# Grouped-query attention on one core: a static instruction plan re-fitted to hand-over times read from a trace

## Chip, cores and metric

The kernel runs on 1 core of a Trainium2 chip. The metric is device time in microseconds (us) for one execution; several executions of each kernel are compared. Runs are "fast" with a granted TensorE clock of 0.995 to 1.0. The time is about 1.8 us longer than the span of a profile (385.81 us against 384.0 in the profiled run of before), so times are compared with times and spans with spans.

## The reference

```
q: (8, 8, 1024, 64), k and v: (8, 2, 1024, 64), float32, randn * 0.1
for each of 2 kv heads g, its 4 query heads:
    scores = q @ k^T / sqrt(64)
    attn   = exp(scores - max); attn = attn / (sum(attn) + 1e-8)
    output = attn @ v
```

There are 128 jobs (batch, query head, half of the queries; 512 queries each), each with 8 blocks of 128 keys: 1024 score tiles of 128 x 512.

## The kernel before

Each score tile is one matmul (0.2155 us apart on TensorE). Its exponential is made in one of two ways. **A tiles** go to ScalarE, two at a time. **D tiles** go to VectorE, one by one, which builds an approximate exponential out of bit operations and corrects ten tiles at once with a chain of four steps: mask ("and", VectorE), line (GpSimd), product and sum (VectorE). Then TensorE multiplies each tile with V (an output block of four matmuls, 0.123 us) and VectorE normalises each finished job. In PSUM there are two double banks for A, two single banks for D, two for outputs.

The order on each engine is fixed at build time. A greedy function simulates the engines with constant costs and always takes the operation that can start first; the sorted list is the program. The split between A and D is not a parameter: it comes out of this simulation.

```
QK, PV, P1, NORM = 0.216, 0.1225, 0.603, 0.555
EXP = (0.05, 0.4268)
FOUR, TWO, POOL_ONE = (0.09, 0.133), (0.05, 0.27), (0.25, 0.43)
COST = {"and": FOUR, "line": POOL_ONE, "prod": TWO, "add": TWO}
FROM_PE, FROM_PV, FROM_ACT, FROM_DVE, FROM_POOL = 0.21, 0.16, 0.165, 0.10, 0.15
LIVE_A, LIVE_D, PENDING, PER_JOB, LEAD, RAMP, AHEAD, FIRST_PV = 28, 5, 16, 2, 6, 6, 0.0, 2.0
AHEAD_D, EXTRA, LAST = 0, 0, 6
...
    if job_a < nj:                      # a score for ScalarE
        t = ...max(pe, bank free, data loaded)
            best = min(best or (INF,), (t - AHEAD, 1, "qk", 0, t))
    if job_d < nj and job_d <= job_a + lead + 1 and pending < PENDING:   # one for VectorE
        if cur or live["D"] < LIVE_D:
            t = max(pe, min(bank), loaded(job_d))
            best = min(best or (INF,), (t - AHEAD_D, 2, "qk", 1, t))
...                                     # output blocks, normalisations, chain steps likewise
        if len(o["cells"]) == A_CELLS[o["slot"]] or ...:
            act = max(act, pe + FROM_PE)
            ops.append((act, "exp", a_id, tuple(o["cells"])))
            act += EXP[0] + EXP[1] * len(o["cells"])
            a_free[o["slot"]] = act + FROM_ACT
```

The constants that begin with FROM are the hand-over times: how long after the end of an engine's step the plan lets another engine use its result. PENDING is the number of D tiles that may be begun and not finished. Transfers on GpSimd's queue are placed by planned time too, out of the way of the chains' line steps:

```
POOL_DMA = 1.0
def at_pool(t, f, *args):
    for first, last in chains:          # planned starts of the line steps
        if first - POOL_DMA < t < last:
            t = last + 0.01
    at(t, f, *args)
...
# cast(): a GpSimd transfer that also waits for the last score issued so far ("pace")
```

The softmax here doesn't subtract the row's maximum and nothing guards it: scores larger than these inputs give would overflow.

Of the kernel before, what the change touches and what calls it, by code (L numbers as in the profile page):

```python
# [19 lines left out]
def part(step, m):  # L20

    n = step[-1]
    return slice(0, m) if not n.isdigit() else slice(m * int(n) // PARTS, m * (int(n) + 1) // PARTS)


def make_plan(nj, nkc):
# [6 lines left out]

    QK, PV, P1, NORM = 0.216, 0.1225, 0.603, 0.555
    EXP = (0.05, 0.4268)
    FOUR, TWO, POOL_ONE = (0.09, 0.133), (0.05, 0.27), (0.25, 0.43)
    COST = {"and": FOUR, "line": POOL_ONE, "prod": TWO, "add": TWO}
    FROM_PE, FROM_PV, FROM_ACT, FROM_DVE, FROM_POOL = 0.21, 0.16, 0.165, 0.10, 0.15
    LIVE_A, LIVE_D, PENDING, PER_JOB, LEAD, RAMP, AHEAD, FIRST_PV = 28, 5, 16, 2, 6, 6, 0.0, 2.0
    INF = 1e9  # L40
    AHEAD_D, EXTRA, LAST = 0, 0, 6
    FIRST_TURN, FIRST_LOAD, EACH_LOAD = 2.4, 4.5, 4.2
# [9 lines left out]
    p1q, chainq, normq, cur = [], [], [], []  # L52
# [4 lines left out]
    def loaded(j):  # L57
        h = j // 2
        if not h:
            return FIRST_TURN * (j % 2)  # L60
        return FIRST_LOAD + EACH_LOAD * (h - 1 if h < 4 else h)

    def first_free(slots):
        return min(range(len(slots)), key=lambda s: slots[s])


    while normed < nj:
        best = None
        while job_a < nj and not todo[job_a]:
            job_a += 1  # L70
        lead = min(LEAD, job_a // RAMP)
        job_d = max(job_d, job_a + lead)
        while job_d < nj and (
            taken[job_d] >= PER_JOB + EXTRA * (job_d >= nj - LAST)
            or not todo[job_d]
        ):
            job_d += 1
        if job_a < nj:
            t = INF
            if open_a is not None:  # L80
                t = max(pe, open_a["t"], loaded(job_a))
            elif live["A"] < LIVE_A:
                t = max(pe, min(a_free), loaded(job_a))
            if t < INF:
                best = min(best or (INF,), (t - AHEAD, 1, "qk", 0, t))
        if job_d < nj and job_d <= job_a + lead + 1 and pending < PENDING:
            if cur or live["D"] < LIVE_D:
                t = max(pe, min(bank), loaded(job_d))
                if t < INF:
                    best = min(best or (INF,), (t - AHEAD_D, 2, "qk", 1, t))  # L90
        for i, s in enumerate(open_jobs):
            for c in rem[s]:
                at = max(pe, FIRST_PV, ready.get(s * nkc + c, INF))
                if at < INF:
                    best = min(best or (INF,), (at, 3 + i, "pv", (s, c)))
        if len(open_jobs) < O_BANKS and next_job < nj:
            at = min(ready.get(next_job * nkc + c, INF) for c in range(nkc))
            at = max(pe, FIRST_PV, min(obank_free), at)
            if at < INF:
                best = min(best or (INF,), (at, 3 + len(open_jobs), "open", next_job))  # L100
        for q, p, kind in ((normq, 0, "norm"), (p1q, 1, "p1")):
            if q:
                best = min(best or (INF,), (max(dve, q[0][0]), p, kind, 0))

        for i, (at, _, _, step) in enumerate(chainq):
            if CHAIN[step] in ON_POOL:
                at = max(at, pool, two_end)
            else:
                at = max(at, dve, pool)
            best = min(best or (INF,), (at, 2 + i, "chain", i))  # L110
        if cur and job_d >= nj and not p1q:
            best = min(best or (INF,), (dve, 9, "flush", 0))
        t, _, kind, arg = best[:4]
        if kind == "qk":
            t = best[4]
            pe = t + QK
            j = job_d if arg else job_a
            cell = j * nkc + todo[j].pop(0)
            if not arg:
                if open_a is None:  # L120
                    slot = first_free(a_free)
                    a_id += 1
                    live["A"] += 1
                    open_a = {"slot": slot, "t": a_free[slot], "cells": []}
                    a_free[slot] = INF
                o = open_a
                ops.append((t, "qk", cell, "A", a_id, o["slot"], len(o["cells"])))
                o["cells"].append(cell)
                home[cell] = ("A", a_id)
                if len(o["cells"]) == A_CELLS[o["slot"]] or not any(todo[job_a:]):  # L130
# [4 lines that stand above are left out]
                    uses[("A", a_id)] = len(o["cells"])  # L135
                    for x in o["cells"]:
                        ready[x] = act + FROM_ACT
                    open_a = None
            else:
                taken[j] += 1  # L140
                k = first_free(bank)
                bank[k] = INF
                pending += 1
                ops.append((t, "qk", cell, "D", k, 0, 0))
                p1q.append((pe + FROM_PE, cell, k))
        elif kind == "open":
            o = first_free(obank_free)
            obank[arg] = o
            obank_free[o] = INF
            open_jobs.append(arg)  # L150
            rem[arg] = list(range(nkc))
            next_job += 1
        elif kind == "pv":
            s, c = arg
            cell = s * nkc + c
            opens = len(rem[s]) == nkc
            rem[s].remove(c)
            done = not rem[s]
            ops.append((t, "pv", s, cell, opens, done, obank[s]))
            pe = t + PV  # L160
            h = home[cell]
            uses[h] -= 1
            if not uses[h]:
                live[h[0]] -= 1
            if done:
                open_jobs.remove(s)
                normq.append((pe + FROM_PV, s))
        elif kind == "norm":
            s = normq.pop(0)[1]
            ops.append((t, "norm", s))  # L170
            dve = t + NORM
            obank_free[obank[s]] = dve + FROM_DVE
            normed += 1
        elif kind == "p1":
            _, cell, k = p1q.pop(0)
            if not cur:
                d_id += 1
                live["D"] += 1
            ops.append((t, "p1", cell, k, d_id, len(cur)))
            dve = t + P1  # L180
            bank[k] = dve + FROM_DVE
            cur.append(cell)
            home[cell] = ("D", d_id)
            if len(cur) == GROUP:
                chainq.append((dve, d_id, cur, 0))
                cur = []
        elif kind == "flush":
            chainq.append((dve, d_id, cur, 0))
            cur = []
        else:  # L190
            _, g, cells, step = chainq.pop(arg)
            ops.append((t, "chain", g, len(cells), CHAIN[step]))
            name = CHAIN[step]
            fixed, each = COST[name.rstrip("0123456789")]
            end = t + fixed + each * len(cells[part(name, len(cells))])
            if name in ON_POOL:
                pool = end
            else:
                dve = two_end = end
            if step + 1 < len(CHAIN):  # L200
                at = end
                if (name in ON_POOL) != (CHAIN[step + 1] in ON_POOL):
                    at += FROM_POOL if name in ON_POOL else FROM_DVE
                chainq.insert(arg, (at, g, cells, step + 1))
            else:
                pending -= len(cells)
                uses[("D", g)] = len(cells)
                for x in cells:
                    ready[x] = dve + FROM_DVE
# [4 lines left out]
def kernel(  # L214
# [40 lines left out]

    jobs = [(b, h, side) for b in range(B) for h in range(H) for side in range(2)]
    plan = make_plan(len(jobs), NKC)
    starts = {}
    for op in plan:
# [391 lines left out]
```

## Time and profile before

| | before |
|---|---|
| time, median (range of 3) | 385.43 us (385.39 to 386.04) |
| span of the profiled run | 384.0 us |
| ScalarE / TensorE / VectorE / GpSimd busy | 98% / 95% / 92% / 45% |
| exponentials on ScalarE, D tiles, chains | 404, 216, 22 |

All three large engines are nearly full.

### The profile page before, as it was taken

What the parts mean: (1) busy time and instruction counts of PE and PEld (TensorE: products, weight loads), DVE (VectorE), ACT (ScalarE), POOL (GpSimd) and SP (SyncE); (2) the same over time, 40 slices, a digit from 0 to 9 for tenths busy, and PEclk for the clock granted to TensorE, in tenths of its full rate; (3) what the DMA queues carried; (4) which work ended last, traced back from release to release, by engine and by line L of the source; (5) the groups of instructions that cost most, each with busy time, mean ns of one, the idle gap of its engine ahead of it and who ended that gap; (6) DMA issues with size and microseconds to landing.
All of it is one profiled execution on the core that took longest, in us unless ns stands there. A gap on an engine that the chain in (4) does not pass through costs nothing.

```text
span 384.0 us, 12026 instructions
## 1 busy us (share of the span) xinstructions
PE 365.6 (95%) x5172; PEld 233.6 (61%) x5172; DVE 353.8 (92%) x548; ACT 374.6 (98%) x409; POOL 174.4 (45%) x147
## 2 busy tenths in 40 slices
PE   8879898999999999999999999999999999998995
PEld 7425464666666666666666666666666666564664
DVE  4779998999999999999999999999999999989982
ACT  5999999999999999999999999999999999999995
POOL 5584535718244371563718245271643627040420
PEclk9999999999999999999999999999999999999999
DMA  8988988697756848585676759468675765711213
GB/s 137 135 152 135 130 154 124 129 147 140 113 109 132 140 103 139 101 156 103 139 131 120 130 106 152 96 126 137 105 124 123 138 102 119 126 56 29 57 56 84
DMA packets 102485, 45.48 MB, mean 118 GB/s; under 512 B 63792, under 2 KB 100976, under 8 KB 101184
## 3 DMA queue, kind: packets, MB, share of 16 engines
q1 hardware_dynamic: 82096, 31.21, 36.1%
q0 software_dynamic: 19712, 13.18, 32.3%
q8 instruction: 40, 0.66, 0.7%
q10 hardware_dynamic: 624, 0.33, 0.3%
q14 instruction: 13, 0.11, 0.1%
HBM read 25.17 MB, written 27.00 MB: 136 GB/s over the span
## 4 chain that ended last, share of the span: by engine, by line
ACT 86%; PE 10%; DVE 2%; issue 1%
ACT p_ring L477 86%; PE aps L466 4%; PE ops L538 4%; PE ops L409 1%; PE dps L466 1%; DVE pd L527 1%; DVE ost L554 0%; DVE y L525 0%; DVE z L512 0%; DVE rec L551 0%; PE dps L382 0%; PE dps L428 0%; PE ops L428 0%; PE aps L382 0%; DVE blank L288 0%
## 5 line engine op out<-in xcount | busy, mean ns | idle before, releaser
L477 ACT ACTIVATE p_ring<-aps 128x1024 bf16<-128x1024 f32 x404 | 371.8, 1067 | 1.4 <-PE aps L466 1.2
L466 PE MATMUL aps<-qT,kset 128*128 128x512 bf16 x808 | 239.9, 378 | 13.0 <-ACT p_ring L477 12.4
L538 PEld LDWEIGHTS <-p_ring 128*128 128x128 bf16 x3232 | 140.1, 98 | 64.0
L538 PE MATMUL ops<-vset,p_ring 128*128 128x65 bf16 x3232 | 154.6, 194 | 0.0
L491 DVE TENSOR_SCALAR pd<-dps 128x512 uint16<-128x512 f32 x216 | 138.6, 683 | 7.0 <-PE dps L466 6.7
L516 POOL TENSOR_SCALAR y<-z 128x5120 f16<-128x5120 uint16 (+1 forms) x22 | 96.4, 4383 | 70.0 <-DVE rec L551 48.7
L466 PEld LDWEIGHTS <-kset 128*128 128x128 bf16 x1024 | 79.7, 97 | 56.4 <-issue 25.8
L323 POOL DMA_DIRECT2D scr_q<-in_q_dram x63 | 39.1, 621 | 83.5 <-PE dps L466 44.3
L466 PE MATMUL dps<-qT,kset 128*128 128x512 bf16 x216 | 76.4, 379 | 0.0
L525 DVE TENSOR_TENSOR y<-z,y 128x5120 f16<-128x5120 uint16 (+1 forms) x22 | 61.0, 2772 | 1.1 <-POOL y L516 1.1
L527 DVE TENSOR_TENSOR pd<-pd,y 128x5120 uint16<-128x5120 uint16 (+1 forms) x22 | 60.9, 2769 | 0.1
L554 DVE TENSOR_TENSOR ost<-ops,rec 128x256 f32<-128x256 f32 x128 | 54.3, 425 | 4.4
L538 PEld LDWEIGHTS <-pd 128*128 128x128 bf16 x864 | 42.8, 98 | 24.7 <-DVE ost L554 2.2
L538 PE MATMUL ops<-vset,pd 128*128 128x65 bf16 x864 | 52.2, 194 | 0.3
L512 DVE TENSOR_SCALAR z<-pd 128x5120 uint16<-128x5120 uint16 (+1 forms) x22 | 32.3, 1467 | 0.5
L551 DVE RECIPROCAL rec<-ops 128x4 f32<-128x4 f32 x128 | 22.6, 176 | 9.6 <-PE ops L538 8.2
L323 POOL DMA_DIRECT2D scr_k<-in_k_dram x15 | 9.8, 656 | 39.9 <-PE aps L466 33.0
L356 POOL DMA_DIRECT2D vset<-in_v_dram x32 | 24.9, 784 | 0.0
L409 PE MATMUL ops<-blank 128*128 128x128 bf16 x40 | 5.3, 313 | 1.1 <-DVE blank L288 1.1
L409 PEld LDWEIGHTS <-blank 128*128 128x128 bf16 x40 | 4.4, 149 | 1.1 <-DVE blank L288 1.1
L363 POOL DMA_DIRECT2D kset<-kset x6 | 4.1, 684 | 0.0
L420 ACT ACT_TABLE_LOAD x1 | 1.3, 1283 | 1.8 <-issue 1.8
(23 smaller groups left out, 10.2 us busy)
## 6 DMA issues: line engine op xcount, KB each, us to landing
out_dram<-ost SPq DMA_DIRECT2D x63, 256.0 KB, 2.9
scr_q<-in_q_dram POOLq DMA_DIRECT2D x63, 128.0 KB, 3.5
kset<-kT SPq DMA_DIRECT2D x60, 64.0 KB, 3.1
vset<-in_v_dram POOLq DMA_DIRECT2D x32, 64.0 KB, 3.9
scr_k<-in_k_dram POOLq DMA_DIRECT2D x15, 128.0 KB, 3.7
qT<-scr_q SPq DMA_TRANSPOSE x63, 3.5
kset<-kset POOLq DMA_DIRECT2D x6, 128.0 KB, 4.3
fq<-in_q_dram ACTq DMA_DIRECT2D x2, 128.0 KB, 3.3
```

The source lines that it names most:

```text
L323: dma = nc.gpsimd.dma_start(out=scr.rearrange("(p f) -> p f", f=1024), in_=src.rearrange("(p s) d -> p (s d)", s=1024 // D),)
L356: nc.gpsimd.dma_start(out=vsets[b % 2][:, g, two * NHC : (two + 1) * NHC, 0:D], in_=v[b, g].rearrange("(c p two) d -> two p c d", p=128, t ...
L466: last_score[0] = nc.tensor.matmul(dst, lhsT=ksets[b % 2][:, h // HPG, side, c * 128 : (c + 1) * 128], rhs=qT[(b, h)], start=True, stop=Tr ...
L477: act = nc.scalar.activation(out=pt[:, 0:m], in_=psum.pop(("A", n))[:, 0:m], func=AF.Exp, scale=scale)
L491: nc.vector.tensor_scalar(out=groups[g][:, slot], in0=psum.pop(cell), scalar1=bits_scale, scalar2=bits_bias, op0=ALU.mult, op1=ALU.add,)
L512: eng.tensor_scalar(out=z, in0=pd, scalar1=0x7F, scalar2=None, op0=ALU.bitwise_and)
L516: eng.tensor_scalar(out=y, in0=z, scalar1=CURVE_A / 128.0, scalar2=CURVE_B, op0=ALU.mult, op1=ALU.add,)
L525: eng.tensor_tensor(out=y, in0=z, in1=y, op=ALU.mult)
L527: eng.tensor_tensor(out=pd, in0=pd, in1=y, op=ALU.add)
L538: nc.tensor.matmul(ops_of[s][:, qs, :], lhsT=p_of[cell][:, qs * 128 : (qs + 1) * 128], rhs=vsets[b % 2][:, h // HPG, c, :], start=opens an ...
L551: nc.vector.reciprocal(out=rec, in_=o[:, :, D])
L554: nc.vector.tensor_tensor(out=stage[(b, h)][:, :, side, :], in0=o[:, :, 0:D], in1=rec.unsqueeze(2).to_broadcast([128, NQS, D]), op=ALU.mult,)
```

## The change

The intent is to let the plan's hand-over times be those that a trace shows between TensorE, VectorE and GpSimd, and to let a ScalarE score wait up to 0.06 us for its bank rather than have TensorE begin something else.

```
-    FOUR, TWO, POOL_ONE = (0.09, 0.133), (0.05, 0.27), (0.25, 0.43)
+    FOUR, TWO, POOL_ONE = (0.20, 0.133), (0.05, 0.27), (0.25, 0.417)
-    FROM_PE, FROM_PV, FROM_ACT, FROM_DVE, FROM_POOL = 0.21, 0.16, 0.165, 0.10, 0.15
-    LIVE_A, LIVE_D, PENDING, PER_JOB, LEAD, RAMP, AHEAD, FIRST_PV = 28, 5, 16, 2, 6, 6, 0.0, 2.0
+    FROM_PE, FROM_PV, FROM_ACT, FROM_DVE, FROM_POOL = 0.21, 0.20, 0.165, 0.135, 0.06
+    LIVE_A, LIVE_D, PENDING, PER_JOB, LEAD, RAMP, AHEAD, FIRST_PV = 28, 5, 16, 2, 6, 6, 0.06, 2.0
-                chainq.append((dve, d_id, cur, 0))
+                chainq.append((dve + 0.11, d_id, cur, 0))        # in both places
```

More of the change, by code (lines that the diff above doesn't have):

```diff
@@ L184, in make_plan @@
             if len(cur) == GROUP:
-                chainq.append((dve, d_id, cur, 0))
+                chainq.append((dve + 0.11, d_id, cur, 0))
                 cur = []
         elif kind == "flush":
-            chainq.append((dve, d_id, cur, 0))
+            chainq.append((dve + 0.11, d_id, cur, 0))
             cur = []
```

## The prediction

> **What bounds the kernel now.** I read the busy line first, then the groups, the chain that ended last, the waits, and last a few microseconds of the timeline.
>
> ```profile
> span 384.0 us, 12026 instructions
> PE 365.6 (95%) x5172; PEld 233.6 (61%) x5172; DVE 353.8 (92%) x548; ACT 374.6 (98%) x409; POOL 174.4 (45%) x147
> ```
>
> ScalarE (ACT) is busy 98% of the span, TensorE 95% and VectorE 92%. Nothing here has much room, so the question is which engine sets the pace and by how much the others disturb it.
>
> ```profile
> L477 ACT ACTIVATE p_ring<-aps 128x1024 bf16<-128x1024 f32 x404 | 371.8, 1067 | 1.4 <-PE aps L466 1.2
> L466 PE MATMUL aps<-qT,kset 128*128 128x512 bf16 x808 | 239.9, 378 | 13.0 <-ACT p_ring L477 12.4
> L491 DVE TENSOR_SCALAR pd<-dps 128x512 uint16<-128x512 f32 x216 | 138.6, 683 | 7.0 <-PE dps L466 6.7
> L516 POOL TENSOR_SCALAR y<-z 128x5120 f16<-128x5120 uint16 (+1 forms) x22 | 96.4, 4383 | 70.0 <-DVE rec L551 48.7
> ```
>
> 404 exponentials of two score tiles each on ScalarE, 216 score tiles on VectorE (808 + 216 = 1024), in 22 chains. ScalarE's idle time is only 1.4 us, but this figure hides something: one exponential lasts 1067 ns and yet 404 of them occupy 371.8 us, 920 ns each, because the next begins before the last has ended. A late score first eats this overlap, and only then appears as idle. From the start times in the trace: the shortest distance between two starts is 0.903 us, half of the 403 distances lie between 0.903 and 0.910, the mean is 0.920. Against 0.905 (my choice for an undisturbed one) the sum of excess is 6.2 us. That is nearly all that better feeding can win at this split.
>
> ```profile
> 105.11 23.81 ACT p_ring L477 x26
> 128.99 23.90 ACT p_ring L477 x26
> 152.93 23.86 ACT p_ring L477 x26
> 176.86 23.80 ACT p_ring L477 x26
> 200.71 23.91 ACT p_ring L477 x26
> ```
>
> In the chain in order of time, runs of 26 exponentials take about 23.86 us, 0.918 each; undisturbed they would take 26 x 0.905 = 23.53. So the loss is spread evenly, 0.3 us in each run. Where it comes from:
>
> ```profile
> 170.34 4.47 POOL L516 TENSOR_SCALAR y<-z 128x5120 f16<-128x5120 uint16 x1
> 170.34 0.42 DVE L554 TENSOR_TENSOR ost<-ops,rec 128x256 f32<-128x256 f32 x1
> 170.59 0.13 PEld L466 LDWEIGHTS <-kset 128*128 128x128 bf16 x2
> 170.62 0.60 PE L466 MATMUL aps<-qT,kset 128*128 128x512 bf16 x2
> 170.68 2.49 DVE L491 TENSOR_SCALAR pd<-dps 128x512 uint16<-128x512 f32 x4
> ...
> 171.05 0.41 PE L538 MATMUL ops<-vset,p_ring 128*128 128x65 bf16 x8
> ...
> 171.41 0.38 PE L466 MATMUL dps<-qT,kset 128*128 128x512 bf16 x1
> 171.63 0.59 PE L466 MATMUL aps<-qT,kset 128*128 128x512 bf16 x2
> ```
>
> TensorE takes its work in the fixed order that the plan chose. The eight output matmuls from 171.05 are issued by 171.30 (0.031 us apart), but the VectorE score behind them starts at 171.41: it waits for its bank, whose reader began at 170.68 and lasts 0.68. This 0.117 us wait holds up the ScalarE pair queued behind, which starts at 171.63, and the exponential on it begins 0.987 us after the one before instead of 0.905. The same pattern returns every 16.5 us, once per VectorE chain: from about 120 to 300 the work is periodic, 18 exponentials and 10 VectorE tiles per round.
>
> [...] independent VectorE tiles start 0.598 us apart though each lasts 0.681, while a dependent mask step starts 0.034 after the end of the tile before, 0.715 after its start. [...] in this trace the product starts 0.03 to 0.07 after GpSimd's end in most chains.
>
> **The change, part by part.** No instruction is added, removed or altered in shape. Only the constants of the planning function change, hence the order on each engine, the split between ScalarE and VectorE, and with the planned times the issue order of some transfers.
>
> 1. A finished group becomes ready for its mask 0.11 later. Real: 0.715 from start of the last tile, plan 0.603, difference 0.112. Right.
> 2. Mask fixed cost 0.09 to 0.20: 0.11 more VectorE time per full chain. The mask lasts 1.49 at ten tiles, planned 1.42 before and 1.53 after.
> 3. VectorE's hand-over 0.10 to 0.135. A bank comes free 0.681 + 0.053 = 0.734 after the reader's start in the trace; planned 0.703, now 0.738. Right.
> 4. GpSimd's line 4.55 to 4.42 and its hand-over 0.15 to 0.06: start to product 4.70 before, 4.48 after; the trace has 4.47 + 0.03 = 4.50.
> 5. The end of a job's last output matmul to normalisation, 0.16 to 0.20: a little later, little effect.
> 6. A ScalarE score may be chosen when its bank is within 0.06 us of being free, though something else could start at once.
>
> For VectorE the chain costs 0.11 (part 1) + 0.11 (part 2) + 0.035 (part 3) - 0.22 (part 4) = +0.035 us longer from last tile to product. Over a 16.4 us round that is 0.2%, half a tile of 216. If only the longer occupation counts and the wait for GpSimd had been filled anyway, it is 0.22 of 16.4, 1.3%, some 3 tiles. So I expect 213 to 217 VectorE tiles, 404 or 405 exponentials: half an exponential more, +0.4 us.
>
> For ScalarE, sort the intervals by when their score pair started. A bank can be written 1.118 us after its exponential began (1.067 + 0.051). The exponential two later is on time if its pair starts by 2 x 0.905 - 0.63 = 1.18, where 0.63 is pair start to exponential start (0.216 + 0.378 + 0.036). So the real tolerance is 0.06 us. 162 of some 400 pairs started over 0.06 after the bank came free and carry 5.7 us of the 6.2 us excess.
>
> - Parts 1 to 3 target the once-per-chain wait: about 0.08 us of delay x 17 affected chains = 1.4 us. The score is planned later or behind the pair. I credit 1.2.
> - Part 6 targets the remaining 5.7 - 1.4 = 4.3 us. Without it TensorE can start a VectorE score (0.216) or an output block (0.123) just before the bank comes free. With it, an output block can overrun by at most 0.063, just tolerated, a score by 0.156. Overruns by scores stay, and the plan's unchanged ScalarE hand-over (0.904 + 0.165 = 1.07 against 1.118) blunts the rule. I credit 40%, 1.7 us.
> - Waiting costs TensorE time: decision points lie some 0.16 us apart, so about 0.06/0.16 of the pairs wait 0.03 on average, 0.011 x 404 = 4.5 us in all. TensorE's real work is 1024 x (0.2155 + 0.123) = 347 us in 377, so most of this fits, but not everywhere. I charge 0.2.
>
> Sum: -1.2 - 1.7 + 0.4 + 0.2 = -2.3 us; 385.4 - 2.3 = 383.1.
>
> **Rivals.** (a) The split moves against the change: VectorE, planned dearer, gets ten tiles fewer, ScalarE five exponentials more, 5 x 0.905 = 4.5 us, and the gain is gone: about 387. For it: its rounds are already nearly full, idle only 7.7 us between 60 and 340. Against it: part 4 gives back what parts 1 to 3 take. (b) The wait is paid elsewhere: TensorE falls behind, output blocks pile up and end in the tail, or the VectorE scores come so late that VectorE idles. It would read 384.5 to 385.5. For it: 95% busy; between 120 and 320 it is busy 196.1 of 200. (c) The repair is complete: every pair in time, excess down to the 1.4 us that even the unhurried intervals show (3.5 ns each), 6.2 - 1.4 = 4.8 us: 380.6. With a few more VectorE tiles, 379. Against it: output blocks and scores don't divide a period evenly. Four blocks and a pair take 0.922 (131 intervals do this), one block and two VectorE scores 0.985 (33), three and one 1.015 (26).
>
> **Range and chances.** 383.1, with (c) setting the lower edge at 380.6 and two or three exponentials more the upper at 385.6. Faster by over 2% means 377.7 or less: 7.7 us, more than the whole excess, so it takes three or more exponentials off ScalarE as well: 4%. Slower by over 2% is 393.1, nine exponentials more: 2%. Within 2%: 94%.
>
> **What would show each step.** Right: the x26 runs shorten to about 23.7 us; no VectorE score waits 0.117 us behind output blocks once per chain; exponential count 403 to 406; TensorE's idle before ScalarE scores spread over more places. Wrong: runs of 26 unchanged (the waits were not the loss); 410 or more exponentials (rival a); or shorter runs with a longer tail after the last exponential, now 384.0 - 379.4 = 4.6 us (rival b). I am least sure of the 40%.

## More of the kernel before

One fact of how exponentials overlap becomes important, and the prediction passes over it. The view by tile shows it: durations in ns, minimum, median, maximum.

```profile
L477 ACT ACTIVATE p_ring<-aps x404: 1018/1067/1152, 7.4 to 378.4; 128x1024 bf16<-128x1024 f32 x135
```

The same instruction on the same shape takes between 1018 and 1152 ns. A reader should ask why before taking any distance of starts for the engine's pace (the time from one instruction to the next when nothing holds it up).

## The result

387.41 us (387.11 to 387.92, 4 runs), against 385.47 us (385.39 to 386.04, 4 runs) before: ratio 1.0049, 95% interval 1.0031 to 1.0066. So it is slower by half a per cent: clearly slower, and outside the predicted range of 380.6 to 385.6. A ratio here is the mean time of one kernel's fast runs over that of the other's fast runs of the same rounds, so it is not quite the ratio of the medians quoted beside it.

The page of the changed kernel, the same lines as shown of before:

```profile
span 385.7 us, 11924 instructions
PE 363.6 (94%) x5079; PEld 233.9 (61%) x5172; DVE 347.4 (90%) x539; ACT 376.2 (98%) x412; POOL 166.1 (43%) x146
...
L477 ACT ACTIVATE p_ring<-aps 128x1024 bf16<-128x1024 f32 x407 | 373.5, 1122 | 1.2 <-PE aps L466 1.2
...
L491 DVE TENSOR_SCALAR pd<-dps 128x512 uint16<-128x512 f32 x210 | 137.2, 683 | 12.2 <-PE dps L466 11.5
L516 POOL TENSOR_SCALAR y<-z 128x5120 f16<-128x5120 uint16 x21 | 93.6, 4459 | 62.7 <-DVE z L512 41.8
```

First, the count: 407 exponentials where there were 404, 210 D tiles where there were 216, 21 chains where there were 22. (93 matmul records are missing in this trace, 5079 of 5172, so TensorE's busy time is not compared.) Second, VectorE lost work although it was there to be had: its idle time before D tiles went from 7.0 to 12.2 us. The table by stretch says the same of the middle, 60 to 340 us, before and then after:

```profile
60.00:340.00 280.00, 273.69 (x3979) 176.35 (x3975) 273.17 (x420) 279.95 (x306) 129.47 (x103) 1.00 0.71 123
```

```profile
60.00:340.00 280.00, 271.58 (x3893) 176.20 (x3965) 266.29 (x410) 280.00 (x307) 122.17 (x100) 1.00 0.76 123
```

The columns are the stretch, its length, then the busy times of TensorE, weight loads, VectorE, ScalarE and GpSimd. VectorE idles 13.7 us of 280 instead of 6.8, while ScalarE was full before and is full after. Third, the chain in order of time, the same stretch as shown of before:

```profile
104.45 23.79 ACT p_ring L477 x26
128.23 0.04 issue
128.28 23.86 ACT p_ring L477 x26
152.14 0.04 issue
152.18 23.72 ACT p_ring L477 x26
175.90 0.04 issue
175.95 23.79 ACT p_ring L477 x26
199.78 23.79 ACT p_ring L477 x26
```

The runs of 26 (counted from one start to the next) did become shorter, but by 0.07 us, not by the 0.16 that I had asked for as the sign of success: from one run's start to the next it is (199.78 - 104.45) / 4 = 23.83 us, or 0.9166 per exponential; before it was (200.71 - 105.11) / 4 = 23.90, or 0.9192. And the view by tile now reads:

```profile
L477 ACT ACTIVATE p_ring<-aps x407: 1018/1138/1152, 6.6 to 379.6; 128x1024 bf16<-128x1024 f32 x136
```

The median duration rose from 1067 to 1138 ns. This is no slowdown. An exponential may start as little as 0.903 us after the one before, but in both kernels, wherever one lasts over 1.03 us (320 of 403 before, 395 of 406 after), it **ends** 0.9167 us after the one before on average, with 90% between 0.915 and 0.918. Starts run ahead of ends by some 0.014 us each time, durations grow from 1.018 towards 1.152, and there it stops, because the next score pair waits until its bank is released: in the trace of before no pair starts less than 0.051 us after the end of the exponential two before it (worked out under experiment 4). A stretch of growing durations is therefore, here, ScalarE at full pace. Counting ends, all of the profiled span comes apart like this:

span = end of the first exponential + (count - 1) x 0.9167 + lost time between ends + tail after the last exponential

| profiled run | count | first end | x 0.9167 | lost | tail | span |
|---|---|---|---|---|---|---|
| before | 404 | 8.43 | 369.43 | 1.58 | 4.60 | 384.0 |
| after | 407 | 7.66 | 372.18 | 0.82 | 5.05 | 385.7 |

"Lost" is the sum over all exponentials of the distance of ends less 0.9167. After, 0.61 of its 0.82 us lies in the first twenty exponentials (the start-up, which varies: first end plus this is 8.43 before, 8.27 after). In the middle the loss went from 1.28 to 0.08 us. So the change did what it was meant to do, feed ScalarE without a gap, and this was worth 1.2 us. Three more exponentials cost 2.75 us, and the tail 0.45.

### The profile page after: what moved, and what is told of

Read it like the earlier page. It is cut to its first block, busy times and chain, and to the rows that moved or that the text cites. A ratio compares the mean times of both kernels' runs of the same rounds, so it can differ in the third digit from the quotient of the medians.

```text
span 385.7 us, 11924 instructions
## 1 busy us (share of the span) xinstructions
PE 363.6 (94%) x5079; PEld 233.9 (61%) x5172; DVE 347.4 (90%) x539; ACT 376.2 (98%) x412; POOL 166.1 (43%) x146
## 4 chain that ended last, share of the span: by engine, by line
ACT 94%; PE 3%; DMA 1%; issue 0%; DVE 0%
ACT p_ring L477 94%; PE ops L538 1%; PE ops L409 1%; DMA kset<-kset 1%; PE aps L466 1%; DVE ost L554 0%; PE dps L466 0%; PE dps L382 0%; PE dps L428 0%; DVE rec L551 0%; DVE blank L288 0%; ACT qT L438 0%; PE aps L382 0%; ACT kset L437 0%
## 5 line engine op out<-in xcount | busy, mean ns | idle before, releaser
L466 PE MATMUL aps<-qT,kset 128*128 128x512 bf16 x725 | 222.4, 378 | 11.3 <-ACT p_ring L477 9.2
L538 PEld LDWEIGHTS <-p_ring 128*128 128x128 bf16 x3256 | 135.9, 97 | 58.7
L538 PE MATMUL ops<-vset,p_ring 128*128 128x65 bf16 x3256 | 148.1, 194 | 2.6
L491 DVE TENSOR_SCALAR pd<-dps 128x512 uint16<-128x512 f32 x210 | 137.2, 683 | 12.2 <-PE dps L466 11.5
L516 POOL TENSOR_SCALAR y<-z 128x5120 f16<-128x5120 uint16 x21 | 93.6, 4459 | 62.7 <-DVE z L512 41.8
L466 PE MATMUL dps<-qT,kset 128*128 128x512 bf16 x206 | 71.5, 379 | 1.8 <-DMA kset<-kset 0.6
L525 DVE TENSOR_TENSOR y<-z,y 128x5120 f16<-128x5120 uint16 x21 | 59.1, 2815 | 1.0 <-POOL y L516 0.9
L527 DVE TENSOR_TENSOR pd<-pd,y 128x5120 uint16<-128x5120 uint16 x21 | 59.1, 2816 | 0.1
L538 PEld LDWEIGHTS <-pd 128*128 128x128 bf16 x840 | 38.6, 97 | 25.6 <-DVE pd L527 4.8
L538 PE MATMUL ops<-vset,pd 128*128 128x65 bf16 x840 | 44.3, 194 | 1.2
L512 DVE TENSOR_SCALAR z<-pd 128x5120 uint16<-128x5120 uint16 x21 | 31.2, 1487 | 0.3
```

The costliest lines, as they stand in the source:

```text
L466: last_score[0] = nc.tensor.matmul(dst, lhsT=ksets[b % 2][:, h // HPG, side, c * 128 : (c + 1) * 128], rhs=qT[(b, h)], start=True, stop=Tr ...
L491: nc.vector.tensor_scalar(out=groups[g][:, slot], in0=psum.pop(cell), scalar1=bits_scale, scalar2=bits_bias, op0=ALU.mult, op1=ALU.add,)
L512: eng.tensor_scalar(out=z, in0=pd, scalar1=0x7F, scalar2=None, op0=ALU.bitwise_and)
L516: eng.tensor_scalar(out=y, in0=z, scalar1=CURVE_A / 128.0, scalar2=CURVE_B, op0=ALU.mult, op1=ALU.add,)
L525: eng.tensor_tensor(out=y, in0=z, in1=y, op=ALU.mult)
L527: eng.tensor_tensor(out=pd, in0=pd, in1=y, op=ALU.add)
```

## The experiments

**Theory P**: ScalarE's own pace is 0.917 us per exponential, the time follows the number of exponentials that the greedy plan happens to give ScalarE, and better feeding (having every score ready in time) was worth little over 1 us. **Rival Q**: the pace is 0.905 as predicted, and the changed kernel lost its gain elsewhere. **Rival R**: one part of the change (hand-overs or preference) is harmful and the other good. To choose experiments I ran the planning function by itself for many sets of constants, and replayed plans with hand-over times from the traces. That is how the expectations know the counts.

### 1 and 2: each part alone

```
# ahead_only: the kernel before with          # handover_only: the changed kernel with
-   ... RAMP, AHEAD ... = ... 6, 0.0, ...     -   ... RAMP, AHEAD ... = ... 6, 0.06, ...
+   ... RAMP, AHEAD ... = ... 6, 0.06, ...    +   ... RAMP, AHEAD ... = ... 6, 0.0, ...
```

> The kernel before with only the 0.06 us preference for ScalarE scores. Its plan has 407 exponentials and 210 VectorE tiles, as the whole change has, against 404 and 216. Theory P (ScalarE really needs 0.917 us for each exponential, so the time follows the count, and better feeding saves at most 1 to 1.5 us): about +1.5 to +2.5 us against before. Rival Q (floor 0.905 as I predicted, feeding is worth up to 5 us and this part supplies 1.7 of it): 3 x 0.905 - 1.7 = about +1 us or less, with exponential starts closer than 0.910 apart in the middle of the run. Rival R (the loss comes from the hand-over constants, not from the preference): no more than +0.5 us.

> The changed kernel with the preference set back to 0: hand-over times and costs alone. Its plan has 408 exponentials and 209 VectorE tiles. Theory P (0.917 us for each exponential): 4 x 0.917 = 3.7 less at most 1.4 us of better feeding, so +2.2 to +3 us against before, slower than the whole change or equal. Rival Q (floor 0.905, the once-per-chain wait worth 1.2 us): about +2.4. Rival R (the hand-over constants alone explain the loss and the preference helps): the slowest of this set by over 1 us.

Measured: the preference alone 387.88 us, ratio 1.0066 (1.0053 to 1.0078); the hand-over times alone 387.57, ratio 1.0055 (1.0043 to 1.0068), both against 385.45 before. Each part alone costs as much as both together, so rival R falls: it is not that one is harmful and the other good. The lost time is 1.12 and 0.23 us, the counts are 407 and 408. The hand-over times alone came out just below their range (+2.1 where +2.2 to +3 was expected). One reason is in the trace: with 209 D tiles the number of A tiles is odd, so the last exponential takes a single tile and ends 0.489 us after the one before in place of 0.917. This makes the lost time of 0.23 us look 0.43 too small; in the middle, which it does not touch, the loss is 0.23 us too.

### 3: the price of three exponentials

```
-        if job_d < nj and job_d <= job_a + lead + 1 and pending < PENDING:
+        if sum(taken) < 210 and job_d < nj and job_d <= job_a + lead + 1 and pending < PENDING:
```

> The kernel before, all its constants kept, but VectorE takes no more tiles after its 210th, so 407 exponentials as in the changed kernel; the order is the same as before's up to there. This measures the price of three exponentials without any change of hand-over times. Theory P: 3 x 0.917 = +2.75 us against before (388.2), 0.5 to 1 us slower than the changed kernel, whose feeding is better. If the count is not what matters, it stays within 0.5 us of before.

Measured: 387.47 us, ratio 1.0058 (1.0045 to 1.0071). In its trace the last exponential ends at 382.21 us, 2.77 later than before (379.44), which is 3 x 0.917; the tail happened to be 0.5 us shorter (4.06), so the profiled spans differ by 2.3 us. The medians differ by 2.0, short of the expected 2.75, and cap210 is not slower than the changed kernel as expected. With no hand-over time changed, moving six tiles back to ScalarE makes the kernel as slow as the change did.

### 4: ScalarE's own pace, with most output work taken from TensorE

```
-        for qs in range(NQS):
+        for qs in range(NQS if opens else 0):     # first of a job's eight output blocks only
```

Its output is wrong, which doesn't matter for the time.

> The kernel before with its plan unchanged (404 exponentials), but only the first of each job's eight output blocks is multiplied, so TensorE has 1024 x 0.2155 + 128 x 0.123 = 236 us of work in place of 347 and every score is in time. The result is wrong on purpose. It measures ScalarE's own pace. Theory P (0.917 us each): first start to last end 404 x 0.917 + 0.1 = 370.6 us, ends of exponentials 0.917 apart throughout, time 383.5 to 384.5. Rival Q (0.905 each, as I predicted from the distances of starts): 365.8 us from first start to last end, time about 379.

Measured: 382.81 us, ratio 0.9935 (0.992 to 0.995). From the first start (7.06) to the last end (377.99) it takes 370.9 us; P said 370.6, Q 365.8. The chain in order of time:

```profile
176.14 23.79 ACT p_ring L477 x26
199.93 0.04 issue
199.98 23.79 ACT p_ring L477 x26
223.76 0.04 issue
223.81 23.79 ACT p_ring L477 x26
```

and the view by tile:

```profile
L477 ACT ACTIVATE p_ring<-aps x404: 1017/1149/1152, 7.1 to 376.8; 128x1024 bf16<-128x1024 f32 x135
  PE aps L466: 66.5, 230
```

The second line stands under "who waited for it": TensorE now waits 230 times for an A bank, 66.5 us in all: the scores wait for ScalarE. And still 26 exponentials take 23.84 us, 0.917 each, and the median duration is 1149 ns.

By itself this leaves a rival. With two A banks, a score pair starts 0.05 us after the end of the exponential two before it (within 0.06 us in 394 of 402 cases here), and its exponential starts 0.63 us after the pair (medians). At a duration of 1.15 us this loop alone gives 1.83 us for two exponentials, 0.917 each. The distances of ends at shorter durations decide it. Exponentials of 1.03 to 1.14 us have not reached that limit (129 in this trace, 289 in that of before), and their starts come as close as 0.903 us in that of before; they too end 0.9167 us after the one before, on average in both traces. So the pace is ScalarE's, the loop only stops the durations from growing, and rival Q falls. All that better feeding could ever win on the kernel before, with its split, is its lost 1.58 us. (The time itself fell 0.7 us below P's range; with no output work after the last exponential the tail is 3.12 us in place of 4.60.)

### 5 and 6: one constant corrected, and five nanoseconds

```
# pool_only: before with                         # p1_5ns: before with
-   ..., POOL_ONE = ..., (0.25, 0.43)            -   QK, PV, P1, NORM = 0.216, 0.1225, 0.603, 0.555
+   ..., POOL_ONE = ..., (0.25, 0.417)           +   QK, PV, P1, NORM = 0.216, 0.1225, 0.598, 0.555
```

> The kernel before with one constant corrected: GpSimd's 0.43 us per tile becomes 0.417[...]. Making GpSimd cheaper in the plan ought to help if the plan's accuracy is what counts (rival: same or up to 0.5 us faster). But its plan has 408 exponentials and 209 VectorE tiles. Theory P (the count times 0.917 us, feeding worth at most 1.4): 4 x 0.917 - 1.4 = +2.3 us at the least, up to +3.5.

> The kernel before with the planned time of a VectorE tile 0.598 us in place of 0.603, five thousandths, and nearer to the 0.598 that the trace shows. Theory P: the kernel before sits on an order that the greedy plan reaches by chance; this plan has 407 exponentials and 211 tiles, and a last VectorE group that is finished later, so +2.5 to +4 us. Rival (what matters is the hand-over times and the preference of the change): no difference from before above 0.5 us.

Measured, with before at 385.77 us: 387.23, ratio 1.0037 (1.0024 to 1.0049), and 388.98, ratio 1.0089 (1.0073 to 1.0104). Two corrections towards the trace, one of them of 5 ns, each made the kernel slower. (In the plan a line step of ten tiles goes from 4.55 to 4.42 us, where the trace of before has 4.45 to 4.48; a VectorE tile goes from 0.603 to 0.598, the distance of starts in that trace. The clause that the trace shows 0.417 us per tile on GpSimd is cut from the expectation: the one line step of six tiles in that trace took 2.75 us, so from six tiles to ten it is 0.43.) The first was milder than expected (+1.5 where +2.3 was the least): its four exponentials cost 3.67 us, less 0.43 because the last takes a single tile, and it got back 0.79 of lost time, 0.44 at the start and 0.38 in the tail. The second has 407 exponentials (the last of a single tile) and a tail of 6.25 us.

The kernel before is a lucky draw. I gave the planning function 300 sets of constants near before's: the hand-over times and the chain's fixed costs within 0.01 us, GpSimd's cost per tile within 0.001. No run records my first draws; a repetition gave 404 exponentials 41 times, 407 most often (115 times), and a range of 404 to 411. Around the changed kernel's constants it was 407 in 267 of 300. With other choices of the constants to be varied, 404 or fewer came out in 13 to 23% of the sets. This says nothing of the chip; it says that "before" was an unusually good outcome of a greedy rule, and that about four in five small changes of its constants would lose it.

### 7 to 10: the constant that was left out, and the limit on open tiles

The change corrects hand-overs of TensorE, VectorE and GpSimd, but not the cost of an exponential, planned at 0.05 + 2 x 0.4268 = 0.904 us. true_act puts this right and raises PENDING; limit18 and act_cost_only do one of the two; best is a further tuned plan.

```
# true_act = the changed kernel with
-   EXP = (0.05, 0.4268)          -  FROM_ACT 0.165        -  PENDING 16
+   EXP = (0.05, 0.4335)          +  FROM_ACT 0.20         +  PENDING 18
# limit18: PENDING alone;  act_cost_only: EXP and FROM_ACT alone
# best: true_act with LEAD 7, EXTRA 2, FOUR (0.14, ..), POOL_ONE (.., 0.43),
#       FROM_PE 0.20, FROM_PV 0.16, FROM_DVE 0.10
```

> The changed kernel with ScalarE's own pace put right as well: 0.05 + 2 x 0.4335 = 0.917 us for an exponential in place of 0.904, its hand-over 0.20 in place of 0.165, and up to 18 VectorE tiles begun and not finished in place of 16. Its plan has 403 exponentials and 218 tiles. Theory P: four exponentials fewer than in the changed kernel, 3.7 us, so 383.7 to 384.7; against before one exponential fewer and about 1 us of better feeding, -0.8 to -1.8 us. If the count is not what sets the time, it stays at the changed kernel's 387.4.

> The same idea, taken from some twelve thousand plans by their replay with the hand-over times of the trace: 403 exponentials, 218 tiles, a shorter end (seven jobs of lead in place of six, VectorE allowed four tiles of each of the last six jobs). Theory P: -1.8 to -2.5 us against before, about 383.2, the fastest here; below 382 only if an exponential costs less than 0.917.

> The changed kernel with one number altered: up to 18 VectorE tiles begun and not finished, in place of 16. All its hand-over times, costs and the preference stay. Its plan has 405 exponentials and 214 tiles. Theory P: two exponentials fewer than in the changed kernel, so its last exponential ends 1.8 us earlier; but the plan closes the last VectorE group late and leaves more output work behind the last exponential, so the time is only 0 to 1.5 us better than the changed kernel's 387.4. If this limit has nothing to do with VectorE's lost tiles, VectorE's idle time in the middle stays where the changed kernel has it.

> The changed kernel with ScalarE's true pace (0.917 us for an exponential) and hand-over (0.20), and the limit left at 16. Its plan has 405 exponentials and 214 tiles. Theory P: -1.8 us from the count against the changed kernel, so about 385.8 to 386.6, at or slightly above before, as the plan that starts from a true pace leaves VectorE its time. If the count doesn't matter: 387.4.

| kernel | count | lost | tail | time | ratio to before (95%) |
|---|---|---|---|---|---|
| true_act | 403 | 0.98 | 5.43 | 384.47 | 0.9963 (0.995 to 0.9975) |
| best | 403 | 2.11 | 4.60 | 384.83 | 0.9976 (0.9963 to 0.9988) |
| limit18 | 405 | 0.62 | 7.40 | 388.44 | 1.0074 (1.0061 to 1.0087) |
| act_cost_only | 405 | 3.15 | 5.92 | 390.02 | 1.0108 (1.0088 to 1.0129) |

The times stand for all runs of a kernel, the three terms for the one that was profiled. In limit18 that was its shortest run (387.71 us). In act_cost_only it took 388.75: three of its six runs took 388.5 to 389.4, the other three 390.6 to 391.2 at a granted clock of 0.995, and no trace shows where the latter lost their time.

The first is as expected: both corrections together bring VectorE's tiles back (218), and VectorE is busy 271.7 us between 60 and 340, nearly as before. The other three missed. They show that the count alone isn't the time; the two other terms of the sum must be watched too. In limit18 the last exponential ends at 378.54, 2.1 us earlier than in the changed kernel, 1.8 of it for the two exponentials fewer, but TensorE is then behind with output blocks and works on for 3.26 us:

```profile
376.93 0.43 PE aps L466 x2
377.37 4.44 PE ops L538 x144
381.83 0.19 DVE rec L551
```

144 output matmuls in a row at the very end: work saved on ScalarE and paid in the tail. The limit explains a part of VectorE's lost work only: between 60 and 340 us it idles 11.9 us here, 13.7 in the changed kernel and 6.8 before. In act_cost_only and best a hole opened in the middle, and the chain of act_cost_only leads to its cause:

```profile
274.13 0.06 issue
274.19 0.05 POOL scr_q L323
274.24 0.48 issue
274.72 4.48 POOL y L516
279.20 0.03 issue
279.22 2.82 DVE y L525
...
282.65 0.65 PE ops L538 x16
283.30 0.45 PE aps L466 x2
```

The line step (POOL y) starts at 274.72, though its mask was ready at 272.75 (271.27 + 1.48). In the other chains of this trace it mostly starts 0.08 to 0.13 us after its mask. Ahead of it in GpSimd's queue stood a transfer that had waited 11.0 us for TensorE. (The program makes such a transfer wait for a score; the view names an output matmul as what released it.) The late chain holds up an output block, which holds up the score pair behind it on TensorE, and an exponential ends 1.62 us late. In this trace GpSimd did not take the line step before the waiting transfer: the step stood ready for 1.97 us behind it.

### 11 and 12: GpSimd's queue kept clear

```
-    POOL_DMA = 1.0
+    POOL_DMA = 3.0
```

> The kernel with ScalarE's true pace and a limit of 16, with one more number altered: no transfer is put on GpSimd in the 3 us before a chain's line step, in place of 1 us. In its first form it took 390.0 where 386 was expected; its trace shows the line step at 274.72 though its input was ready at 272.75, behind a transfer that had waited 11.0 us on GpSimd for a score and started at 274.19, and then an exponential 1.62 us late. Theory G (a paced transfer holds GpSimd's queue, the chain's output is late and TensorE waits for it): the hole goes, 387 to 388.4. If the hole has another cause: still 389.5 or more.

> The plan with 403 exponentials and the short end, with the same 3 us in place of 1. In its first form it fell 1 us short of the expectation; its trace has the line step at 269.86 with its input ready at 268.10, behind a transfer that waited until 269.33, and an exponential 0.93 us late. Theory G: about 0.9 to 1.2 us better than its first form, 383.4 to 384.0 where before is 385.5, the fastest of all. If the hole has another cause: 384.8 as in its first form.

Measured, with before at 385.52 us: 386.49, ratio 1.0027 (1.0014 to 1.0041), and 383.40, ratio 0.9938 (0.9925 to 0.995). With no change to the plans, only to where transfers stand in GpSimd's queue, the lost time fell from 3.15 to 0.78 us and from 2.11 to 0.07, and no line step after the first of the run starts more than 0.11 us after its mask. The first did even better than expected, but its gain of 3.5 us in the medians is more than its trace shows: the profiled spans differ by 1.7 us. Against the three faster runs of act_cost_only (388.75 in the median) it is 2.3 us. The second is the fastest kernel here, 2.1 us (0.6%) under before, and correct. Its ScalarE is full from the first exponential to the last: 7.83 + 402 x 0.9167 + 0.07 + 4.59 = 381.0 us. From here the time falls only with fewer exponentials on ScalarE, or a shorter start or end.

## Why the prediction was wrong

Two steps failed, and the split weighed more. The predicted sum was -2.3 us, the profiled spans differ by +1.7. Of these 4.0 us the count of exponentials makes 2.35 (+2.75 in place of +0.4), the gain from feeding 1.7 (1.2 in place of 2.9) and the tail 0.25; the start and the last 25 exponentials took 0.34 off.

- **What bounds the kernel.** Right in kind: ScalarE sets the pace. The step that failed here is "Against 0.905 (my choice for an undisturbed one) the sum of excess is 6.2 us. That is nearly all that better feeding can win at this split." The pace is 0.9167, measured on ends in both kernels and in light_pe, and the true loss was 1.58 us. I had seen durations of 1067 ns at distances of 920 and explained them by overlap, but did not ask why they ranged from 1018 to 1152. Taking starts for the pace counted full-speed stretches as delay: 403 x 0.0117 = 4.7 of the 6.2 us.
- **The gains from parts 1 to 3 and 6.** The mechanism was right: late scores were delaying exponentials, and in the middle of the changed kernel they do so no longer. Its size was wrong. I credited 1.2 + 1.7 = 2.9 us; the middle had only 1.28 to give and gave 1.20. Which part supplied how much of it can't be split cleanly: each alone left 0.47 (preference) or 0.23 us (hand-overs) in the middle, so either alone does most of it. The 162 late pairs are a misreading besides: I took a mean duration for every exponential. Counted from each one's own end they are 141, with 5.2 of the 6.2 us.
- **The split.** "So I expect 213 to 217 VectorE tiles, 404 or 405 exponentials" failed: 210 and 407, so +2.75 us in place of +0.4. I added up VectorE's planned cost per chain (+0.035 us), as though the split were a smooth function of cost. It is the outcome of a greedy order. Rival (a) named the right danger with the wrong size and cause: VectorE did not become too dear; it idled, 13.7 us in place of 6.8 between 60 and 340, waiting for scores (24 waits of 11.5 us in all before D tiles, in place of 9 of 6.7). The 7.7 us of idle time that I gave for before should have read 6.8. That the measured 387.4 is (a)'s "about 387" is chance: (a) had five exponentials more, and the runs three. And dearness is not needed: pool_only, which makes the plan's GpSimd cheaper and nothing dearer, loses even more tiles (209). The count could have been had without a chip: the planning function alone gives 407 and 210 for the changed constants, and I reasoned about it in place of running it. The cost of 0.905 that I gave each extra exponential was close to the measured 0.917.
- **TensorE's waiting and rival (b).** I charged 0.2 us; the tail grew by 0.45, with output work ending 0.92 us after the last exponential in place of 0.48. Small here, it was the decisive term in limit18.
- **The sum.** -1.20 in the middle, +2.75 for the count, +0.45 for the tail, -0.16 for the start and -0.18 in the last 25 exponentials make +1.66, against 385.7 - 384.0 = 1.7 of the profiled spans; the medians differ by 1.94.
- **The signs I named.** Runs of 26 at 23.7 us: they read 23.79, and the experiment with a light TensorE shows that this is as short as they get. A count of 403 to 406: missed by one. The once-per-chain wait of a D score can't be counted in the changed kernel, since its trace lacks 93 matmul records, but the traces of its two parts are complete. Between 20 and 360 us, 13 D scores before stood 0.11 to 0.12 us behind output blocks, and 13 in cap210; in ahead_only and handover_only none did. And TensorE's stalls before ScalarE scores did spread: 101 of over 0.01 us before (100 in cap210), 194 in ahead_only and 133 in handover_only, 20.5, 22.9 and 23.9 us in all (starts, less the usual distance to the matmul before). So the waits that I had aimed at went away as described. They were worth less than I thought.

What stays open: why the greedy rule lands on 404 in one place and 407 beside it was not traced step by step; the runs show only that VectorE idles more, that the outcome changes with 5 ns, and that corrections of ScalarE's cost together with two more open tiles bring it back.

## What to carry to other kernels

Take an engine's pace from the distances between the ends of its instructions, and check it once with its supplier made light, before pricing what better feeding could win; here durations that grew from 1.03 to 1.15 us at a constant 0.917 us between ends marked a full engine. When a change only alters the constants of a greedy plan, run the planner first and compare what it decides (the split, the order of queues, the work left at the end), because a truer constant can give a worse plan. Look also at what stands before a compute step in its queue: in two kernels here a line step on GpSimd stood ready for 1.97 and 1.76 us behind a transfer that waited for TensorE, and with the transfers moved out of its way the lost time fell from 3.15 to 0.78 and from 2.11 to 0.07 us. Write the time as a sum of count x pace, lost time and tail, and judge every variant by all three.
